# Turning the last two heads' attention probabilities by TensorE transposes instead of DMA transposes

## The chip, the cores and the metric

One core of one Trainium2 chip runs the whole program in one launch. The metric is the device time in microseconds (us) of one execution; a time is the median of several runs. A profile is one further execution, recorded by the hardware profiler; its times count from the start of its span. In the profile PE is TensorE (PEld its weight loads), DVE is VectorE, ACT is ScalarE, POOL is GpSimd and SP is SyncE, whose queue issues most DMAs.

## The reference

Two layers work on 256 tokens and 256 context tokens of width 2048, in float32. Layer 0 is a Fourier mixer, layer 1 an attention. The change lies in the attention, which for each of 64 query heads (8 per key head, head width 64) computes

```python
s = einsum('bqhgd,bkhd->bhgqk', q, k) * 64 ** -0.5
s = where(mask, s, NEG_INF)                # 256 own keys in a window, 256 context keys
p = softmax(concatenate([s, sink], -1))[..., :-1]
o = einsum('bhgqk,bkhd->bqhgd', p, v)
y = o * silu(z)
x = x + gate * (y @ w_out[1])              # then a final rmsnorm
```

The product with the values contracts over keys, while the softmax leaves a tile with queries on partitions. So each head's probabilities have to be turned before the second product. That is 512 keys by 256 queries for each head.

## The kernel before

**Precision.** A float32 product is done as three products of high and low parts (`mm3`, lines 77 to 80: lines 78, 79 and 80 of the profile). `split` (lines 64 to 66) makes the parts: ACT casts the high part (line 65), DVE or POOL subtracts for the low part (line 66). Probabilities and values are split into two float16 parts instead.

**One head.** `stage_s(i)` (from line 1141) computes the scores of head i for two blocks of 128 queries (lines 1154 and 1155), masks and reduces them on DVE (line 1156), exponentiates on ACT (line 1159), and writes for each block a float16 tile `f` of 128 queries by 1024, namely 512 high parts by ACT (line 1166) and 512 low parts by DVE (line 1167). Line 1168 then has SP issue one DMA transpose per block, which writes the turned tile `ft`. Tiles `f` have three buffers, and so do the tiles `ft`. `stage_o(i)` (from line 1171) multiplies by the values with 8 matmuls of 256 columns (lines 1176 and 1177), which need both blocks of `ft`; ACT and DVE take the result out (lines 1182 and 1183), and after every second head `emit_y` (line 1139) makes one block of y.

**The loop.** Head i's scores are issued two iterations ahead of its `stage_o`. Between them `filler()` issues units of other PE work: q and z projections (lines 1118 and 1120), and at the end the first 12 of 16 weight pieces of the output projection's first quarter (`o1_step`, from line 984; weights `wo1a`). That quarter reads y split in high and low parts by `y_split` (from line 976): blocks 0 to 15 into `ys` tiles of one pool, blocks 16 to 23 into tiles of the pool `act` with POOL subtracting, blocks 24 to 31 into `ys` tiles of the last stage's pool with DVE subtracting. After the loop come the last four weight pieces (lines 1246 to 1249), the exit of that quarter (`evac`, lines 1235 to 1244, which needs the gate row `gbc` and the residual tiles `x2`), and then the quarters with the weights `wo1b` and `wo1c`.

**What sets the order.** The kernel is written in a tile framework that places instructions by a model of its own: each engine's order is fixed when the program is built, and need not be that of the source. A tile's pool decides which buffer it gets. The pool `act` has 33 buffers of 128x512 float32, and at the end of the attention it holds y, the values, the parts of y's blocks 16 to 23, and the eight residual tiles `x2`, which POOL loads by DMA at line 1228. The rows `gbc` (line 1223) and `fg` (line 1230) are loaded by POOL's queue too. Weights arrive through three `raw` buffers of 1 MB (line 49), issued on SP's queue, the queue of the DMA transposes.

Of the kernel before, what the change touches and what calls it, by code (L numbers as in the profile page):

```python
# [12 lines left out]
F16 = mybir.dt.float16  # L13
# [4 lines left out]
P = 128  # L18
# [13 lines left out]
def tile_dit(ctx: ExitStack, tc: tile.TileContext, a: dict, out: bass.AP):  # L32
    nc = tc.nc
    V, S, PE, GP = nc.vector, nc.scalar, nc.tensor, nc.gpsimd
# [4 lines left out]
    actp = ctx.enter_context(tc.tile_pool(name="act", bufs=33))  # L39
    pp = ctx.enter_context(tc.tile_pool(name="ps", bufs=8, space=bass.MemoryType.PSUM))  # L40
    dram = ctx.enter_context(tc.tile_pool(name="dram", bufs=1, space=bass.MemoryType.DRAM))

    def psum():
        return pp.tile([P, 512], F32, tag="ps", name="ps")

    def raw(src, q=None):
        t = rawp.tile([P, D], F32, tag="raw", name="raw")
        n = src.shape[-1]
        last_dma[0] = (q or nc.sync).dma_start(t[:, :n], src).ins
        return t  # L50
# [3 lines left out]
    def act(dt=F32):  # L54
        return actp.tile([P, 512], dt, tag="act", name="act")
# [21 lines left out]
    def mm3(o, wh, wl, xh, xl, start, stop):  # L77
        PE.matmul(o, wh, xh, start=start, stop=False)  # L78
        PE.matmul(o, wh, xl, start=False, stop=False)  # L79
        return PE.matmul(o, wl, xh, start=False, stop=stop).ins  # L80
# [19 lines left out]
    ident = const.tile([P, P], F32, name="ident")  # L100
# [598 lines left out]
    with tc.tile_pool(name="yp", reuse_waits="tile", bufs=32) as ypool:  # L699
# [20 lines left out]
        with tc.tile_pool(name="zp", reuse_waits="tile", bufs=2) as zp:  # L720
# [30 lines left out]
            for b in range(4, NB):  # L751
# [3 lines left out]
                o = psum()  # L755
# [41 lines left out]
        for i in range(32):  # L797
            sw, kg = i // 16, i % 16
            if kg == 0:
                o = [psum() for _ in range(8)]  # L800
# [6 lines left out]
            if kg >= 12:  # L807
                for k in range(sw * 8 + (kg - 12) * 2, sw * 8 + (kg - 12) * 2 + 2):
                    t = act()
# [41 lines left out]
    with tc.issue_after(st_end[0]):  # L851
        o = psum()
# [34 lines left out]
    with tc.tile_pool(name="h1", reuse_waits="tile", bufs=16) as h1p:  # L887
# [4 lines left out]
        with tc.tile_pool(name="kvp", reuse_waits="tile", bufs=2) as kvp:  # L892
# [3 lines left out]
            for k in range(KT):  # L896
                hx = h1p.tile([P, 512], F32R, tag="h1", name="h1")
                hc = kvp.tile([P, 512], F32R, tag="h1c", name="h1c", bufs=16)
                t = kvp.tile([P, 512], F32, tag="ht", name="ht")
# [14 lines left out]
            o = [[psum() for _ in range(2)] for _ in range(4)]  # L914
# [13 lines left out]
            for tb in range(4):  # L928
                t, ab = act(), act(F32R)
# [3 lines left out]
                t = act()  # L933
# [18 lines left out]
            for tb in range(4):  # L952
                t = vs[tb][0]
# [10 lines left out]
        with tc.tile_pool(name="at", reuse_waits="tile", bufs=2) as at:  # L964
# [19 lines left out]
            def o1_step(k, os_, wh, wl):  # L984
                while len(yh) <= min(k + 4, NB - 1) and (len(yh) < 24 or fin):
                    y_split(len(yh))
                for tb in range(2):
                    mm3(os_[tb], yh[k][:, tb * P : (tb + 1) * P], yh[k][:, N + tb * P : N + (tb + 1) * P], wh, wl, k == 0, k == NB - 1)
            slot = [0]

            def k_turn(hp):
                o = psum()
                for tb in range(4):
                    PE.transpose(o[:, tb * P : (tb + 1) * P], kr[tb][:, hp * P : (hp + 1) * P], ident)
                t = act()
                S.copy(t, o)
                kT.append(t)
# [135 lines left out]
            def emit_y(blk):  # L1133
                if blk not in szs or (blk, 1) not in obs or blk in ydone:
                    return
                ydone.add(blk)
                if blk % 2 == 0:
                    y1.append(act())
                V.scalar_tensor_tensor(y1[blk // 2][:, (blk % 2) * N : (blk % 2 + 1) * N], obs[blk, 1], dsc[:, blk // 4 : blk // 4 + 1], szs.pop(blk), op0=ALU.mult, op1=ALU.mult)

            def stage_s(i):
                hk, blk, hh = i // 8, i // 2, i % 2
                p2, pr = (blk % 4) // 2, blk % 2
                kkh, kkl = kk[hk]
                q2 = qq[hk, p2][hh]
                pt = [at.tile([P, 512], F32, tag="p", name="p", bufs=3) for _ in range(2)]
                mx = at.tile([P, 2], F32, tag="mx", name="mx")
                sm = at.tile([P, 2], F32, tag="sm", name="sm")
                es = at.tile([P, 2], F32, tag="es", name="es")
                so = []  # L1150
                for tb in range(2):
                    o = psum()
                    st = q2[:, (pr * 2 + tb) * P : (pr * 2 + tb + 1) * P]
                    PE.matmul(o, st, kkh, start=True, stop=False)  # L1154
                    PE.matmul(o, st, kkl, start=False, stop=True)  # L1155
                    V.tensor_tensor_reduce(o, o, mask[:, tb, :], -0.125, nsink[:, i : i + 1], ALU.add, ALU.min, mx[:, tb : tb + 1])  # L1156
                    so.append(o)
                for tb in range(2):
                    S.activation(pt[tb], so[tb], AF.Exp, bias=mx[:, tb : tb + 1], scale=-1.0, accum_out=sm[:, tb : tb + 1])  # L1159
                S.activation(es, mx, AF.Exp, bias=sink[:, i : i + 1])  # L1160
                V.scalar_tensor_tensor(sm, sm, 1.0 / PS, es, op0=ALU.mult, op1=ALU.add)
                V.reciprocal(sm, sm)
                ft = at.tile([P, 8, 2, P], F16, tag="ft", name="ft", bufs=3)
                for tb in range(2):
                    f = at.tile([P, 1024], F16, tag="f", name="f", bufs=3)
                    S.activation(f[:, 0:512], pt[tb], AF.Copy, scale=sm[:, tb : tb + 1])  # L1166
                    V.scalar_tensor_tensor(f[:, 512:1024], pt[tb], sm[:, tb : tb + 1], f[:, 0:512], op0=ALU.mult, op1=ALU.subtract)  # L1167
                    nc.sync.dma_start_transpose(ft[:, :, tb, :], f)
                return ft

            def stage_o(i, ft):
                hk, blk, hh = i // 8, i // 2, i % 2
                oo = psum()
                for kb in range(4):
                    fh, fl = (ft[:, j, :, :].rearrange("p t q -> p (t q)") for j in (kb, 4 + kb))
                    PE.matmul(oo[:, 0:N], v01[kb][:, hk, :], fh, start=kb == 0, stop=False)  # L1176
                    PE.matmul(oo[:, 0:N], v01[kb][:, hk, :], fl, start=False, stop=kb == 3)  # L1177
                if hh == 0:
                    obs[blk, 0] = at.tile([P, N], F32, tag="ob", name="ob", bufs=4)
                ob = obs[blk, 0]  # L1180
                t = at.tile([64, N], F32, tag="ot", name="ot", bufs=1)
                S.copy(t, oo[64:128, 0:N])
                V.tensor_tensor(ob[hh * 64 : hh * 64 + 64, :], oo[0:64, 0:N], t, op=ALU.add)
                if hh == 1:
                    obs[blk, 1] = ob
                    emit_y(blk)
# [13 lines left out]
            def filler():  # L1200
                j = slot[0]
                slot[0] += 1
                emit_unit()
                if defer and defer[0][0] + 2 < j:
                    defer.pop(0)[1]()

            pts = {}
            for i in range(66):
                if i % 8 == 0:
                    while defer:  # L1210
                        defer.pop(0)[1]()
                if i < 64:
                    pts[i] = stage_s(i)
                filler()
                if i >= 2:
                    stage_o(i - 2, pts.pop(i - 2))
                filler()


        with tc.tile_pool(name="fin", reuse_waits="tile", bufs=1) as fp:  # L1220
# [31 lines left out]
            o = [[psum() for _ in range(2)] for _ in range(2)]  # L1252
# [12 lines left out]
            o = [psum() for _ in range(2)]  # L1265
# [34 lines left out]
            for kg in range(8):  # L1300
                t = raw(a["wo1c"][kg])
# [133 lines left out]
```

## Time and profile before

| | |
|---|---|
| median of 3 runs | 1819.78 us (1818.48 to 1819.86) |
| the profiled execution | 1817.29 us, span 1815.5 us |
| PE busy | 1768.6 us, 97% |
| DVE busy | 1412.0 us, 78% |
| ACT busy | 896.9 us, 49% |
| POOL busy | 212.4 us, 12% |
| DMA moved | 399.91 MB, mean 220 GB/s |
| attention's DMA transposes | 128, from 1167.4 to 1643.7 us, median 4.9 us from issue to landing |

A row of the timeline gives an instruction's start, how long it took, its engine, line and tiles, and in brackets how long the engine stood idle before it and what ended that. A row of the windows gives for a stretch of time the busy time of engines, the TensorE clock that was granted (PEclk, 1.00 is full) and the DMA rate. The page's slices are 45.4 us each.

### The profile page before, as it was taken

To read this page: it belongs to the slowest core of one execution; us is meant where nothing else is said; L and a number is where in the kernel's file an instruction comes from. 1 tells how busy PE (TensorE), PEld (TensorE's weight loads), DVE (VectorE), ACT (ScalarE), POOL (GpSimd) and SP (SyncE) were. 2 spreads that over 40 slices of the span, in tenths; PEclk is the share of its full clock that TensorE was granted. 3 is DMA by queue.
4 is the path that set the end of the run, shared out by engine and by line. 5 is a ranking of instruction groups with operands and counts; after the bars stand their busy time and mean duration, and the time that the engine had idled before them with its cause. 6 is when DMAs were issued, how large, how long until landed. Compare 5 with 4: busy or idle time off the path is not lost. (4 is left out here: it accounts for less than half of the span.)

```text
span 1815.5 us, 25987 instructions
## 1 busy us (share of the span) xinstructions
PE 1768.6 (97%) x9417; PEld 1480.2 (82%) x9417; DVE 1412.0 (78%) x2759; ACT 896.9 (49%) x1540; POOL 212.4 (12%) x213
## 2 busy tenths in 40 slices
PE   6999999999999999999999999999999999997998
PEld 4679999888888888888888888788878888875886
DVE  5679888786878887776875654899999999985455
ACT  5545454532222233324322534687778888874343
POOL 0001122100000000000001000402302231161001
PEclk9999999999999999999999999999999999998999
DMA  9988889665767647663567323587988888986553
GB/s 395 417 331 234 231 239 255 216 228 224 252 228 262 244 168 295 229 237 121 186 230 293 119 93 116 162 206 196 224 203 195 215 223 211 213 219 194 188 182 139
DMA packets 209472, 399.91 MB, mean 220 GB/s; under 512 B 156288, under 2 KB 156688, under 8 KB 174272
## 3 DMA queue, kind: packets, MB, share of 16 engines
q1 hardware_dynamic: 185280, 360.24, 61.7%
q0 software_dynamic: 19920, 31.06, 7.0%
q10 hardware_dynamic: 4144, 6.95, 1.1%
q8 instruction: 74, 1.21, 0.3%
q14 instruction: 54, 0.44, 0.1%
HBM read 352.06 MB, written 12.59 MB: 201 GB/s over the span
## 5 line engine op out<-in xcount | busy, mean ns | idle before, releaser
L65 ACT CAST wh<-raw 128x1024 fp32r<-128x1024 f32 x333 | 348.7, 1048 | 531.9 <-PE ps L79 431.1
L66 DVE TENSOR_TENSOR wl<-raw,wh 128x1024 fp32r<-128x1024 f32 x333 | 430.5, 1296 | 220.1 <-ACT wh L65 217.7
L79 PE MATMUL ps<-act,wh 128*128 128x512 f32 x1024 | 398.2, 389 | 0.0
L78 PE MATMUL ps<-act,wh 128*128 128x512 f32 x1024 | 393.8, 389 | 0.0
L80 PE MATMUL ps<-act,wl 128*128 128x512 f32 x1024 | 392.9, 389 | 0.0
L80 PEld LDWEIGHTS ps<-act,wl 128*128 128x128 f32 x1024 | 192.3, 188 | 39.8
L79 PEld LDWEIGHTS ps<-act,wh 128*128 128x128 f32 x1024 | 192.3, 188 | 39.8
L78 PEld LDWEIGHTS ps<-act,wh 128*128 128x128 f32 x1024 | 192.3, 188 | 39.7
L1118 PE MATMUL ps<-h,wh 128*128 128x512 f32 x512 | 185.5, 398 | 0.0
L686 DVE CUSTOM_DVE_ANT_0 raw<-raw,cb 128x512 f32<-128x512 f32 x256 | 172.4, 688 | 11.6 <-DMA raw<-in_adw 8.0
L686 DVE CUSTOM_DVE_ANT_0 junk<-raw,cb 128x512 f32<-128x512 f32 x192 | 131.8, 686 | 32.8 <-DMA raw<-in_adw 21.9
L1120 PE MATMUL ps<-h,wl 128*128 128x256 f32 x512 | 138.9, 281 | 0.0
L79 PE MATMUL ps<-wl,h 128*128 128x512 f32 x320 | 127.1, 397 | 0.4 <-DVE wl L66 0.4
L80 PE MATMUL ps<-wh,h 128*128 128x512 f32 x320 | 125.3, 395 | 0.0
L78 PE MATMUL ps<-wh,h 128*128 128x512 f32 x320 | 124.0, 402 | 0.0
L1167 DVE SCALAR_TENSOR_TENSOR f<-p,sm,f 128x512 f16<-128x512 f32 x128 | 102.9, 821 | 16.4 <-ACT f L1166 16.0
L1118 PEld LDWEIGHTS ps<-h,wh 128*128 128x128 f32 x512 | 96.6, 189 | 19.1
L1166 ACT ACTIVATE f<-p,sm 128x512 f16<-128x512 f32 x128 | 88.1, 717 | 41.5 <-DMA ft<-f 21.6
L1159 ACT ACTIVATE p<-ps,mx 128x512 f32<-128x512 f32 x128 | 87.9, 688 | 38.1 <-DVE mx L1156 31.6
L1120 PEld LDWEIGHTS ps<-h,wl 128*128 128x128 f32 x512 | 97.0, 190 | 2.8
L1156 DVE CUSTOM_DVE_ANT_0 ps<-ps,mask,nsink 128x512 f32<-128x512 f32 x128 | 93.4, 749 | 1.8 <-PE ps L1155 1.6
L1176 PE MATMUL ps<-ft,v 128*128 128x256 f16 x256 | 60.6, 277 | 19.7 <-DMA ft<-f 19.3
(334 smaller groups left out, 3394.9 us busy)
## 6 DMA issues: line engine op xcount, KB each, us to landing
raw<-in_wz SPq DMA_DIRECT2D x64, 1024.0 KB, 5.5
raw<-in_adw SPq DMA_DIRECT2D x64, 1024.0 KB, 5.2
raw<-in_awp SPq DMA_DIRECT2D x32, 1024.0 KB, 12.8
raw<-in_wo SPq DMA_DIRECT2D x32, 1024.0 KB, 6.1
raw<-in_wq SPq DMA_DIRECT2D x32, 1024.0 KB, 5.3
raw<-in_wu SPq DMA_DIRECT2D x32, 1016.0 KB, 6.2
raw<-in_wo1b SPq DMA_DIRECT2D x16, 1024.0 KB, 4.9
act<-in_xT POOLq DMA_DIRECT2D x32, 256.0 KB, 6.3
```

The costliest lines, as they stand in the source:

```text
L65: last_cast[0] = S.copy(h, src).ins
L66: last_sub[0] = eng.tensor_tensor(l, src, h.bitcast(F32), op=ALU.subtract).ins
L78: PE.matmul(o, wh, xh, start=start, stop=False)
L79: PE.matmul(o, wh, xl, start=False, stop=False)
L80: return PE.matmul(o, wl, xh, start=False, stop=stop).ins
L686: V.tensor_tensor_reduce(junk if s == 0 and i < 3 else wf, wf, cb[:, s, kq * 512 : kq * 512 + 512], 1.0, 0.0, ALU.mult, ALU.add, acc[:, i, ...
L1118: PE.matmul(o[0], wh[:, q], hx1[k], start=k == 0, stop=k == KT - 1)
L1120: PE.matmul(o[0][:, 0:N], wl[:, q], hx1[k][:, 0:N], start=False, stop=False)
L1156: V.tensor_tensor_reduce(o, o, mask[:, tb, :], -0.125, nsink[:, i : i + 1], ALU.add, ALU.min, mx[:, tb : tb + 1])
L1159: S.activation(pt[tb], so[tb], AF.Exp, bias=mx[:, tb : tb + 1], scale=-1.0, accum_out=sm[:, tb : tb + 1])
L1166: S.activation(f[:, 0:512], pt[tb], AF.Copy, scale=sm[:, tb : tb + 1])
L1167: V.scalar_tensor_tensor(f[:, 512:1024], pt[tb], sm[:, tb : tb + 1], f[:, 0:512], op0=ALU.mult, op1=ALU.subtract)
```

## The change

For heads 62 and 63 the DMA transposes are left out. Instead `stage_t`, issued two iterations after the head's scores, ahead of its `stage_o`, turns the float16 tile in pieces of 128x128 by 16 TensorE transposes, 8 for each block, into a float16 PSUM tile for each block; ACT copies the first block's to `ft`, DVE the second's. The identity for this, in float16, is copied once by ACT. The four `f` tiles of these heads and the identity are taken from the pool `act`, not from the three buffers of `f`. Heads 0 to 61 are turned as before.

```diff
             slot = [0]
+            ident16 = []
...
                 ft = at.tile([P, 8, 2, P], F16, tag="ft", name="ft", bufs=3)
+                fs = []
                 for tb in range(2):
-                    f = at.tile([P, 1024], F16, tag="f", name="f", bufs=3)
+                    if i < 62:
+                        f = at.tile([P, 1024], F16, tag="f", name="f", bufs=3)
+                    else:
+                        f = actp.tile([P, 1024], F16, tag="act", name="f")
+                        fs.append(f)
                     S.activation(f[:, 0:512], pt[tb], AF.Copy, scale=sm[:, tb : tb + 1])
                     V.scalar_tensor_tensor(f[:, 512:1024], pt[tb], sm[:, tb : tb + 1], f[:, 0:512], op0=ALU.mult, op1=ALU.subtract)
-                    nc.sync.dma_start_transpose(ft[:, :, tb, :], f)
-                return ft
+                    if i < 62:
+                        nc.sync.dma_start_transpose(ft[:, :, tb, :], f)
+                return ft, fs
+
+            def stage_t(ft, fs):
+                for tb in range(2):
+                    o = pp.tile([P, 8, P], F16, tag="ps", name="ps")
+                    for j in range(8):
+                        PE.transpose(o[:, j, :], fs[tb][:, j * P : (j + 1) * P], ident16[0])
+                    (S.copy if tb == 0 else V.tensor_copy)(ft[:, :, tb, :], o)
 
-            def stage_o(i, ft):
+            def stage_o(i, ft, fs):
...
+                if i == 62:
+                    t = actp.tile([P, 1024], F16, tag="act", name="ident16")
+                    ident16.append(t[:, 0:P])
+                    S.copy(ident16[0], ident)
                 if i < 64:
                     pts[i] = stage_s(i)
+                if i - 2 >= 62:
+                    stage_t(*pts[i - 2])
                 filler()
                 if i >= 2:
-                    stage_o(i - 2, pts.pop(i - 2))
+                    stage_o(i - 2, *pts.pop(i - 2))
```

In the built program the order of the engines changes with it, from about head 59 on. On PE, `stage_o` of head 61 stood behind 16 matmuls of the output projection that follow head 63's scores; now it follows those scores directly, and then come 12 of head 62's 16 transposes. The order from there is 10 matmuls, 4 transposes, 14 matmuls, `stage_o` of head 62, 8 transposes of head 63, 4 matmuls, the other 8, `stage_o` of head 63, and the remaining 20 matmuls on `act` tiles. On ACT the casts that split y's blocks 16 to 19 now stand behind head 62's line 1166, and those of blocks 20 to 23 behind head 63's; those of blocks 16 to 21 stood together ahead of both, and only the last two behind head 63's. On POOL the eight loads of `x2` now stand behind the splits of blocks 16 to 19 and ahead of those of blocks 20 to 23; seven of them stood behind the splits of 16 to 21. On SP the weight load that stood between the transposes of heads 62 and 63 follows the last `wo1a` load directly.

## The prediction

> **What bounds the kernel now.** I read the page first: which engine the slices fill, and who makes the chain that ended last.
>
> ```profile
> PE   6999999999999999999999999999999999997998
> PEclk9999999999999999999999999999999999998999
> ...
> PE 16%; DVE 4%; DMA 2%; ACT 1%; issue 1%; SPq 0%; POOLq 0%; DVEq 0%; POOL 0%; ACTq 0%
> ```
>
> PE is full in every slice but a few. The 37th (1634 to 1679 us), where the attention ends, shows 7 and the only dip of the clock, and DMA has a place in the chain. So the waits of this stretch come next, then PE's timeline and its windows.
>
> ```profile
> PE ps L1176 <- DMA ft<-f: 16.2, 2, 12.9
> ```
>
> ```profile
> 1629.14 0.28 PE L1176 MATMUL ps<-ft,v 128*128 128x256 f16 x1 [3.39 <-DMA ft<-f]
> ...
> 1629.92 0.27 PE L1177 MATMUL ps<-ft,v 128*128 128x256 f16 x1
> ...
> 1633.25 0.59 PE L78 MATMUL ps<-wh,act 128*128 128x512 f32 x1
> ...
> 1657.44 0.40 PE L1176 MATMUL ps<-ft,v 128*128 128x256 f16 x1 [12.86 <-DMA ft<-f]
> ...
> 1661.82 0.39 PE L78 MATMUL ps<-wh,ys 128*128 128x512 f32 x1
> ```
>
> From 1560 to 1665 us PE waited twice for transposes: 3.39 us ahead of head 60's `stage_o` and 12.86 us ahead of head 63's, the last. The first and last of head 60's eight matmuls start 0.78 us apart: 0.111 us each. At 1633.25 head 63's scores have just gone; at 1661.82 the first part of y's last blocks is used.
>
> ```profile
> 1169.45:1172.87 3.42, 1.41 (x12) 1.00 0.92 211
> 1172.87:1176.28 3.41, 3.41 (x12) 0.50 0.95 284
> 1623.43:1626.84 3.41, 2.33 (x11) 1.00 1.09 310
> 1626.84:1630.25 3.41, 1.11 (x9) 1.00 1.14 275
> 1630.25:1633.66 3.41, 3.41 (x9) 0.50 1.64 268
> 1657.44:1661.59 4.15, 4.15 (x15) 0.57 0.86 361
> 1661.59:1800.00 138.41, 138.41 (x598) 1.00 0.48 168
> ```
>
> The columns are the stretch, its length, PE's busy time, the clock, DMA. Two things follow. A stretch of 3.4 us in which PE was busy for only 1.41 or 1.11 us is followed by one at half clock, one with 2.33 us is not. Such a slow stretch costs 3.41 x 0.5 = 1.7 us of PE work; the one behind head 63 costs 4.15 x 0.43 = 1.8. So each long wait costs 1.7 us more than its length. And from 1661.59 to 1800 PE is busy without a gap, a 512-column matmul each 138.41 / 598 = 0.231 us: what is won ahead of this is won at the end, one for one.
>
> **Why the two waits exist.** SP's queue, POOL's queue, and three answers about landings: heads 59, 60 and 63, in this order.
>
> ```profile
> 1619.89 6.57 SPq L1168 DMA_TRANSPOSE ft<-f  x2
> ...
> 1627.28 5.37 SPq L1168 DMA_TRANSPOSE ft<-f  x2
> ```
>
> ```profile
> 1609.36 7.29 POOL L66 TENSOR_TENSOR act<-act 128x256 fp32r<-128x256 f32 x6
> 1616.60 3.82 POOL L1228 DMA_DIRECT2D act<-x1d  x7
> ...
> 1645.69 0.56 POOL L1223 DMA_DIRECT2D gbc<-gated  x1
> ```
>
> ```profile
> DMA to landing us min/median/max: 3.3/3.5/3.7
> ```
>
> ```profile
> DMA to landing us min/median/max: 7.0/7.6/8.3
> ```
>
> ```profile
> DMA to landing us min/median/max: 6.0/9.8/13.7
> ```
>
> Head 59's transposes have no POOL load beside them and land after 3.3 to 3.7 us. Head 60's are issued from 1619.89, when seven `x2` loads have just gone out from 1616.60, and take 7.0 to 8.3. Head 63's share the engines with the eighth `x2` load and with `gbc` and `fg`; the later takes 13.7. Where POOL's loads run beside them, transposes take two to four times as long.
>
> **The change, part by part.**
>
> *Head 63's wait goes:* 12.86 us, and the slow stretch behind it, 1.7. No cover is lost; what is late next is the copy out of PSUM, below.
>
> *Head 60's wait goes, though its DMA stays.* The five tiles taken from `act` (four `f`, one identity) push the splits of y's blocks 16 to 23 back. POOL's `x2` loads stand behind the first four splits, those behind ACT casts, and these behind head 62's line 1166, which ran 10 us after head 60's second transpose had gone out:
>
> ```profile
> 1622.14 4.32 SPq L1168 DMA_TRANSPOSE ft<-f  x1
> ```
>
> ```profile
> 1632.54 0.72 ACT L1166 ACTIVATE f<-p,sm 128x512 f16<-128x512 f32 x1 [0.93 <-ACT p L1159]
> ```
>
> Head 60's transposes then land like head 59's, by 1622.1 + 3.5 = 1625.6 at the latest, when PE reaches them (1629.14 - 3.39 = 1625.75). Gain 3.39 + 1.7 = 5.1 us. Bounds: 0, if the `x2` loads are not the cause, and 5.1. I take 5.1, the nearest row being head 59's.
>
> *Head 61's wait is new.* Its `stage_o` loses the 16 matmuls that covered it (16 x 0.231 = 3.7 us) and follows head 63's scores directly, at 1633.25 - 5.1 = 1628.15.
>
> ```profile
> 1625.12 0.75 DVE L1167 SCALAR_TENSOR_TENSOR f<-p,sm,f 128x512 f16<-128x512 f32 x1
> 1628.29 0.72 ACT L1166 ACTIVATE f<-p,sm 128x512 f16<-128x512 f32 x1 [5.19 <-DMA ft<-f]
> ```
>
> The first row is head 61's first block, done at 1625.87; the second block waited 5.19 us for the buffer of head 60's transposes, which now comes free in time. So its low parts follow at 1626.6 to 1627.5, and its transpose goes out at about 1627.7. With head 59's 3.5 us it lands at 1631.2 or so: a wait of 2.9 us with PE busy for some 1.4 of 3.4 us, hence one slow stretch, 1.7. Bounds of the wait: 1.6 (out at 1626.5, 3.3 us) and 8 (8.3 us as head 60's were). Behind the waiting matmul stand all of head 62's transposes and the projection; ACT and DVE work on.
>
> *32 transposes are added on PE.* The trace has float32 ones:
>
> ```profile
> 1552.63 0.60 PE L1037 MATMUL ps<-ident,act 128*128 128x128 f32 x4
> ```
>
> Four in 0.60 us with a tail of 0.27: (0.60 - 0.27) / 3 = 0.11 apart. Float16 has no row for this shape; head 60's matmuls, which load a float16 128x128 each too, are 0.111 apart. 32 x 0.11 = 3.5 us, all on PE's path, as PE has no gaps to put them in but those counted here. From below 0.8 of that (2.8), from above twice (7).
>
> *Copies.* Head 62's lie beside 14 matmuls (3.2 us): nothing. Head 63's `stage_o` stands directly behind its last transpose, so PE waits for DVE's copy of 128x1024 out of PSUM. No such row exists; the nearest are
>
> ```profile
> L65 ACT CAST wh<-raw 128x1024 fp32r<-128x1024 f32 x333 | 348.7, 1048 | 531.9 <-PE ps L79 431.1
> L66 DVE TENSOR_TENSOR wl<-raw,wh 128x1024 fp32r<-128x1024 f32 x333 | 430.5, 1296 | 220.1 <-ACT wh L65 217.7
> ```
>
> 1.05 to 1.3 us, and 0.2 for the transposes to end. DVE also has a line 66 and a line 1183 ahead of the copy, which may end late by as much as one of them. Bounds 1.3 to 2.6; I take 2.0.
>
> *ACT's identity copy and the moved casts* cost nothing: ACT had idle time here (5.19 us ahead of the row above at 1628.29), and the first of blocks 16 to 23 is used only behind head 62's transposes. If its split on POOL comes late, PE waits by the 0.9 us of a split or two.
>
> *Loads.* The four left-out DMAs free SP; PE meets `gbc` and the `wo1b` loads some 10 us earlier.
>
> ```profile
> gbc<-gated POOLq DMA_DIRECT2D x1, 1024.0 KB, 12.7
> fg<-in_fg POOLq DMA_DIRECT2D x1, 1024.0 KB, 16.4
> ```
>
> ```profile
> 1672.62 1.40 DVE L1239 TENSOR_TENSOR act<-ps,gbc 128x512 f32<-128x512 f32 x2
> ```
>
> `gbc` landed at 1645.69 + 12.7 = 1658.4 and would be wanted at 1672.6 - 9.6 = 1663.0: hidden with 4.6 us to spare. 1.8 MB of `x2` now come nearer to it, but the transposes that ran beside it are gone.
>
> *Sum.* Gone: 12.9 + 1.7 + 3.4 + 1.7 = 19.7 us. Added: 3.5 + 2.9 + 1.7 + 2.0 = 10.1. The difference is 9.6 us. From the profiled execution's 1817.3 us (span 1815.5 and 1.8 around it) that makes 1807.7. The median of the three runs, 1819.8, lies 2.5 above that execution; by it the forecast is **1810.2 us**.
>
> **The rivals.**
>
> *Transposes do not hold the clock up.* In the forecast they count as PE work. If not, the stretches after head 61's wait and after head 63's transposes fall under 1.4 of 3.4 us, and two more slow stretches follow: 2 x 1.7 = 3.4, so 1813.6 us. For it: head 63's 16 transposes stand directly before a wait. Against it: nothing, as this trace has no long run of transposes next to a wait. [...]
>
> *The second `wo1b` load is late.*
>
> ```profile
> 1647.33 0.53 SPq L49 DMA_DIRECT2D raw<-in_wo1b  x1
> ```
>
> ```profile
> DMA to landing us min/median/max: 15.0/15.0/15.0
> ```
>
> ```profile
> 1673.03 1.05 ACT L65 CAST wh<-raw 128x1024 fp32r<-128x1024 f32 x1 [1.76 <-PE ps L79]
> ```
>
> This load went out amid `gbc` and `fg`, took 15.0 us and was wanted only at 1673, by ACT's cast. Now it goes out when the last weight pieces are split, at about 1652, and is wanted at about 1663, 11 us later. At 15.0 us PE stops 4 us: 1814.2. Against it: later loads of this kind run alone, and `fg` should be in by then.
>
> *No change.* Head 60's wait stays (5.1) and head 61's runs to 8 us (5.1 more): 10.2 us against a gain of 9.6, so 1820.4. This is the case in which the `x2` loads have nothing to do with the landings.
>
> *Slower: the POOL loads, now together, starve `gbc`.*
>
> ```profile
> 1648.00:1652.00 4.00, 0.00 (x0) 0.00 (x0) 0.00 (x0) 0.00 (x0) 0.00 (x0) 0.50 1.47 122
> ...
> 1656.00:1660.00 4.00, 2.56 (x11) 1.93 (x12) 0.23 (x1) 0.64 (x2) 0.00 (x0) 0.50 0.93 383
> ```
>
> `x2`, `gbc`, `fg` and the first `wo1b` load are 5.2 MB, issued from about 1636. At the first row's 122 GB/s they take 43 us, and `gbc`, if it shares to the end, lands at 1679, 16 us behind its time. DVE stands at line 1239 with the weight splits queued behind it, and PE runs dry: 16 - 9.6 = 6.4 us lost, 1826. It decides from `gbc` landing 9.6 us late. Against it: the low rate belongs to the stretch in which head 63's transposes were in flight; 383 GB/s follow once they are landing, in the second row.
>
> That the change doesn't do what it says is excluded: the two heads have no DMA left.
>
> **How the numbers follow.** Forecast 0.66 (1805.5 to 1815 by the bounds of its terms), clock 0.10, late load 0.10, no change 0.07, slower 0.07. A measurement of this kernel tells 0.2%, about 3.6 us, from no change. The first three cases are faster by more: 0.86. Same 0.07, slower 0.07. The range 1805.5 to 1817 takes in the first three and leaves the last two out.
>
> **What would show it.** Line 1176 of head 63 waits about 2 us for DVE's copy, not 12.9 for a DMA; head 60's waits under 0.5 us and lands in under 5; head 61's waits about 3; POOL's loads at line 1228 start after 1630; the transposes are 0.11 us apart; one slow stretch rather than two. It is wrong if head 60 still waits, if head 61 waits for more than 5, or if PE stops between the last `act` matmul and `wo1c`.

## The result, and the profile after

The changed kernel takes **1803.43 us** (median of 4 runs, 1801.37 to 1805.47); the kernel before, run beside it, 1819.13 us (4 runs, 1814.29 to 1819.86). The ratio is 0.9919, with a 95% interval of 0.9901 to 0.9938. The profiled execution took 1801.37 us with a span of 1799.6, against 1817.29 and 1815.5 before: 15.9 us less. The forecast was 1810.2 (1805.5 to 1817), a gain of 9.6: the sign was right, the gain too small by 6, and the time lies under the range.

The page after, PE's slices, the clock, and the chain that ended last:

```profile
PE   6999999999999999999999999999999999999998
...
PEclk9999999999999999999999999999999999999999
...
PE 21%; ACT 1%; DVE 0%; DMA 0%; issue 0%; POOLq 0%; POOL 0%; DVEq 0%; ACTq 0%
```

The dip in the 37th slice is gone from PE and from the clock, and DMA has fallen from 2% to 0% of the chain. PE's waits from 1560 to 1665 us:

```profile
PE ps L1190 <- DVE ft L1183: 0.9, 1, 0.9
PE ps L1190 <- DMA ft<-f: 0.3, 1, 0.3
```

They were 16.2 us; now they are 1.2. The timeline of PE shows where (line 1190 is the first matmul of `stage_o`, line 1182 the transposes, line 1183 the copies):

```profile
1625.46 0.28 PE L1190 MATMUL ps<-ft,v 128*128 128x256 f16 x1
...
1628.93 0.27 PE L1190 MATMUL ps<-ft,v 128*128 128x256 f16 x1 [0.34 <-DMA ft<-f]
...
1629.80 0.83 PE L1182 MATMUL ps<-ident,f 128*128 128x128 f16 x12
...
1637.23 0.61 PE L1182 MATMUL ps<-ident,f 128*128 128x128 f16 x8
...
1638.66 0.62 PE L1182 MATMUL ps<-ident,f 128*128 128x128 f16 x8
...
1640.22 0.28 PE L1190 MATMUL ps<-ft,v 128*128 128x256 f16 x1 [0.94 <-DVE ft L1183]
```

Head 60 no longer waits, head 61 waits 0.34 us for its DMA, head 63 0.94 us for DVE's copy. Eight transposes take 0.61 us and twelve 0.83: 0.055 us from one to the next, where the forecast put 0.11. The landings of head 60's and head 61's DMA transposes, and of the eight `x2` loads, which now go out from 1632.7:

```profile
DMA to landing us min/median/max: 3.1/3.1/3.2
```

```profile
DMA to landing us min/median/max: 3.1/3.2/3.3
```

```profile
DMA to landing us min/median/max: 4.2/6.1/9.6
```

Head 60's had been 7.0 to 8.3. What the forecast did not have shows in the windows of 1609.40 to 1616.60 us, in which the kernel before ran six splits on POOL. First before, then after; the columns are the stretch, its length, then PE, PEld, DVE, ACT and POOL busy, each with its number of instructions, then the clock, the DMA share and GB/s:

```profile
1609.40:1616.60 7.20, 7.20 (x36) 5.82 (x33) 7.20 (x8) 4.85 (x12) 7.20 (x6) 1.00 0.78 206
```

```profile
1609.40:1616.60 7.20, 7.20 (x36) 5.91 (x34) 7.18 (x16) 5.17 (x13) 0.74 (x2) 1.00 0.90 251
```

DVE was busy throughout in both, but with POOL busy for only 0.74 us, not 7.20, it got 16 instructions done, not 8. The work from one head's line 1156 to the next head's took it 8.9 us before (1607.28 to 1616.22), and after, with one instruction more in it, 6.7 (line 1157, 1608.06 to 1614.74). Its groups in this stretch, before and (0.8 us later) after:

```profile
L66 DVE TENSOR_TENSOR wl<-raw,wh 128x1024 fp32r<-128x1024 f32 x2 | 3.4, 1758 | 0.0
L1167 DVE SCALAR_TENSOR_TENSOR f<-p,sm,f 128x512 f16<-128x512 f32 x2 | 1.9, 990 | 0.0
L1139 DVE SCALAR_TENSOR_TENSOR act<-ob,dsc,th 128x256 f32<-128x256 f32 x1 | 1.0, 964 | 0.0
...
L1161 DVE SCALAR_TENSOR_TENSOR sm<-sm,es 128x2 f32<-128x2 f32 x1 | 0.7, 687 | 0.0
L1183 DVE TENSOR_TENSOR ob<-ps,ot 64x256 f32<-64x256 f32 x1 | 0.4, 406 | 0.0
```

```profile
L66 DVE TENSOR_TENSOR wl<-raw,wh 128x1024 fp32r<-128x1024 f32 x3 | 3.6, 1219 | 0.0
L1173 DVE SCALAR_TENSOR_TENSOR f<-p,sm,f 128x512 f16<-128x512 f32 x3 | 2.2, 746 | 0.0
...
L1140 DVE SCALAR_TENSOR_TENSOR act<-ob,dsc,th 128x256 f32<-128x256 f32 x1 | 0.5, 481 | 0.0
L1197 DVE TENSOR_TENSOR ob<-ps,ot 64x256 f32<-64x256 f32 x1 | 0.4, 414 | 0.0
...
L1162 DVE SCALAR_TENSOR_TENSOR sm<-sm,es 128x2 f32<-128x2 f32 x1 | 0.2, 155 | 0.0
```

The same weight split took 1.76 us beside a busy POOL and 1.22 beside an idle one, the low parts of `f` 0.99 and 0.75, the product in `emit_y` 0.96 and 0.48, and an instruction on two columns (`sm`) 0.69 and 0.155. Each lost 0.24 to 0.54 us, the one on two columns (0.53) as much as the one on 1024 (0.54), so it looks more like a wait for each instruction than a lower rate. The sum into `ob`, which reads one operand from PSUM, took 0.41 both times. The four that were slowed have two inputs in SBUF; why a busy POOL slows them is not shown. The prediction had no term for it.

### The profile page after: what moved, and what is told of

Its sections match the earlier page's. It is cut to its first block, busy times and chain, and to the rows that moved or that the text cites. A ratio compares the mean times of both kernels' runs of the same rounds, so it can differ in the third digit from the quotient of the medians.

```text
span 1799.6 us, 26039 instructions
## 1 busy us (share of the span) xinstructions
PE 1765.1 (98%) x9449; PEld 1478.0 (82%) x9449; DVE 1411.3 (78%) x2761; ACT 898.3 (50%) x1543; POOL 213.5 (12%) x213
## 5 line engine op out<-in xcount | busy, mean ns | idle before, releaser
L79 PE MATMUL ps<-wl,ys 128*128 128x512 f32 (+1 forms) x192 | 75.2, 392 | 0.0
```

## The experiments

The theory behind them: what costs is a DMA transpose in flight beside a load; whatever separates the two wins the same time, and the 6 us that were not forecast come from DVE, freed of POOL's splits. The rival: the gain belongs to TensorE's turning and goes by the heads turned.

| run | median, us | range (runs) | ratio to before | 95% interval |
|---|---|---|---|---|
| `e1_x2_late` | 1804.09 | 1801.15 to 1806.25 (4) | 0.9919 | 0.9903 to 0.9936 |
| `e2_pe_turn_only` | 1808.63 | 1808.03 to 1809.37 (4) | 0.9945 | 0.9931 to 0.9960 |
| `e3_act_tiles_only` | 1819.08 | 1811.88 to 1833.66 (10) | 1.0009 | 0.9985 to 1.0032 |
| `e4_head63_only` | 1803.60 | 1802.82 to 1804.09 (4) | 0.9922 | 0.9906 to 0.9939 |
| `e5_twice` | 1801.71 | 1800.73 to 1807.88 (4) | 0.9905 | 0.9889 to 0.9922 |
| `e6_change_x2_late` | 1802.37 | 1800.93 to 1803.40 (5) | 0.9915 | 0.9900 to 0.9930 |
| `e7_x2_late_loads_held` | 1805.52 | 1803.77 to 1806.85 (6) | 0.9932 | 0.9917 to 0.9947 |
| `e8_pool_busy` | 1806.52 | 1804.31 to 1807.82 (6) | 0.9938 | 0.9924 to 0.9952 |
| `e9_dma_loads_sorted` | 1799.93 | 1799.61 to 1801.07 (4) | 0.9903 | 0.9885 to 0.9921 |
| `e10_change_loads_sorted` | 1801.80 | 1801.29 to 1803.61 (5) | 0.9913 | 0.9897 to 0.9929 |
| `e11_change_again` | 1803.00 | 1800.28 to 1806.16 (6) | 0.9919 | 0.9902 to 0.9935 |

The kernel before had medians of 1818.10, 1818.21 and 1817.74 us beside e1, e2, e3 and e5, beside e4 and e6 to e8, and beside e9 to e11.

### e8: POOL kept busy

The changed kernel, with POOL writing the low part of y's block 15 six times more; the values are the same.

```diff
+                if k == 15:
+                    for _ in range(6):
+                        GP.tensor_tensor(t[:, N : 2 * N], y1[k // 2][:, (k % 2) * N : (k % 2 + 1) * N], t[:, 0:N].bitcast(F32), op=ALU.subtract)
                 yh.append(t)
```

> The changed kernel with six more subtractions on POOL, the same result written again behind y's block 15 (128x256 each), where the kernel before had six splits and the changed kernel has an idle POOL; no other instruction moves. Theory (DVE runs slower beside a busy POOL, and this is why head 61's low parts came some 2 us earlier than forecast): DVE's line 66 goes back from 1.22 towards 1.76 us and line 1173 from 0.75 towards 0.99 in those 7 us, head 61's second transpose goes out 1.5 to 2.5 us later, its wait rises from 0.3 to 2 or 3 us, and a slow stretch of 3.4 us may follow: 1805 to 1808 us. Rival (POOL's work does not matter to DVE, the head start came from the shorter order on ACT alone): head 61 goes out as before, wait under 0.6, 1803.4 us as the changed kernel.

It took 1806.52 us, 3.5 above the changed kernel (1803.00 in e11). The ranges of their runs overlap (1804.31 to 1807.82 and 1800.28 to 1806.16), so the profile has to decide. DVE's groups from 1610.2 to 1617.4, then PE's waits:

```profile
L66 DVE TENSOR_TENSOR wl<-raw,wh 128x1024 fp32r<-128x1024 f32 x2 | 3.4, 1753 | 0.0
L1176 DVE SCALAR_TENSOR_TENSOR f<-p,sm,f 128x512 f16<-128x512 f32 x2 | 1.9, 988 | 0.0
```

```profile
PE ps L1193 <- DMA ft<-f: 3.0, 1, 3.0
PE ps L1193 <- DVE ft L1186: 0.9, 1, 0.9
```

and the stretch behind head 61's wait, with the clock in the last column but two:

```profile
1631.40:1634.80 3.40, 2.94 (x21) 2.44 (x21) 3.37 (x7) 2.59 (x6) 3.40 (x4) 0.50 0.74 284
1634.80:1638.20 3.40, 3.40 (x11) 2.73 (x10) 0.33 (x1) 1.88 (x4) 3.40 (x7) 0.58 0.40 100
```

DVE is back at 1.75 and 0.99 us, within 0.01 us of what it took in the kernel before. Head 61's second transpose goes out at 1628.56 instead of 1625.66, its wait is 3.0 us instead of 0.3, and the clock falls to half behind it. The forecast's wait for head 61 was 2.9. That e8 comes so close to it is in part luck: in e8 DVE starts head 61's low parts at 1626.42, 1.3 us later than in the kernel before (1625.12), from whose times the forecast was made. In e8 and in the changed kernel alike the second transpose goes out 2.14 us behind that start. By this an estimate for DVE's times of before is an issue at 1627.3, a landing 3.1 us later and, with PE there at 1628.6 as in the changed kernel, a wait of some 1.8 us. The theory holds, that a busy POOL makes DVE, and by it head 61's transpose, late; the rival is out.

### e5: each transpose twice

```diff
-                        PE.transpose(o[:, j, :], fs[tb][:, j * P : (j + 1) * P], ident16[0])
+                        for _ in range(2):
+                            PE.transpose(o[:, j, :], fs[tb][:, j * P : (j + 1) * P], ident16[0])
```

> The changed kernel with each of its 32 transposes done twice into the same place; the result is the same. It prices a transpose on PE's path. By the changed kernel's trace (12 in 0.83 us, 0.06 us each) 32 more cost 1.9 us; by the prediction's 0.11 us they cost 3.5 us; if they were hidden beside other waits, 0 to 1 us.

The 32 further transposes cost nothing that the median shows (1801.71 us); by their spacing they are worth 1.8, within the scatter. The profiled execution, at 1807.88 the longest of the four, is of use for another reason. PE's timeline, and its windows around a stretch at half clock:

```profile
1630.59 0.83 PE L1183 MATMUL ps<-ident,f 128*128 128x128 f16 x12
...
1641.46 0.28 PE L1191 MATMUL ps<-ft,v 128*128 128x256 f16 x1 [2.20 <-DVE ft L1184]
...
1642.72 3.21 PE L1183 MATMUL ps<-ident,f 128*128 128x128 f16 x32
```

```profile
1638.45:1641.88 3.43, 1.23 (x8) 0.72 (x7) 3.43 (x3) 1.04 (x2) 2.84 (x5) 1.00 0.93 311
1641.88:1645.30 3.42, 3.42 (x31) 3.15 (x30) 1.07 (x2) 1.00 (x2) 0.00 (x0) 0.51 1.03 426
1645.30:1648.70 3.40, 2.61 (x23) 2.19 (x22) 1.16 (x3) 1.05 (x3) 0.00 (x0) 0.99 1.00 424
```

A wait leaves PE busy for 1.23 of 3.43 us, and half clock follows. That half-clock stretch holds 0.84 us of `stage_o` and then nothing but transposes, and full clock comes back right after it. With only the 0.84 us counted it would have been below the 1.11 and 1.41 of the prediction's rows, which led to half clock. Nor does half clock end by itself after 3.4 us: in e7, below, a stretch at half clock with PE busy for 2.07 us is followed by another. So in this trace the float16 transposes count as PE work for the clock.

### e3: the tiles moved, the turning left to the DMA

The kernel before, with the tiles of heads 62 and 63 and one for the identity taken from `act` as in the change.

```diff
-                    f = at.tile([P, 1024], F16, tag="f", name="f", bufs=3)
+                    if i < 62:
+                        f = at.tile([P, 1024], F16, tag="f", name="f", bufs=3)
+                    else:
+                        f = actp.tile([P, 1024], F16, tag="act", name="f")
...
+                if i == 62:
+                    t = actp.tile([P, 1024], F16, tag="act", name="ident16")
+                    S.copy(t[:, 0:P], ident)
```

> The kernel before with heads 62 and 63 writing f into act tiles and with the identity's act tile, but turned by DMA as all others. Theory: the splits and the x2 loads move back as in the changed kernel, head 60 doesn't wait, head 61 waits under 1 us, and the gain of that half is 5 us or somewhat more; head 63's transposes now run beside all of POOL's loads, so its wait is 12.9 us or up to 4 more. In all 1 to 5 us below the kernel before, 1814 to 1818. Rival (the act tiles do nothing): as before, with head 60's wait.

Without the TensorE transposes the tiles from `act` gain nothing, where 1 to 5 us had been expected: 1819.08 us, and 22 us between the best and the worst of ten runs. PE's waits in the profiled execution (1833.66 us, the longest of the ten), how long head 63's two transposes took to land, and a stretch in the middle of it:

```profile
PE ps L1179 <- DMA ft<-f: 33.1, 3, 32.0
```

```profile
DMA to landing us min/median/max: 26.6/29.0/31.3
```

```profile
1643.80:1660.00 16.20, 0.00 (x0) 0.00 (x0) 0.00 (x0) 0.00 (x0) 0.00 (x0) 0.50 1.31 84
```

Head 63's transposes went out at 1634.91 and 1638.27, amid the eight `x2` loads (from 1632.2), with `gbc` and `fg` behind them. For 16 us no engine did anything, while the DMA engines showed themselves busy and moved 84 GB/s. So taking the tiles from `act` brings the `x2` loads down onto the last head, and the TensorE turning is what makes that harmless. By the medians the turning is worth some 15 us against this kernel.

### e1: only the loads moved

The kernel before, every head turned by the DMA, with the `x2` loads behind POOL's last split.

```diff
+                if k == 23:
+                    gp_sub[0] = last_sub[0]
...
-                    nc.gpsimd.dma_start(x2[tb][c], x1d[tb, :, c * 512 : (c + 1) * 512])
+                    with tc.issue_after(gp_sub[0]):
+                        nc.gpsimd.dma_start(x2[tb][c], x1d[tb, :, c * 512 : (c + 1) * 512])
```

> The kernel before with one edit: POOL issues the eight x2 loads behind the last of its splits (after about 1643 us) instead of at 1616.6. All turning stays with the DMA and the splits of blocks 16 to 21 stay early. Theory (x2 loads are what made head 60's transposes late): head 60's transposes land in under 5 us instead of 7.0 to 8.3, its wait of 3.4 us and the slow clock stretch behind it go, 5 us. Head 63's transposes then share the DMA with all eight x2 loads, so its wait stays at 12.9 us or grows by up to 4. In all 0 to 5 us below the kernel before. Rival (head 60 was late because DVE and POOL were slowed by the splits, not by DMA traffic): the landing of head 60's transposes stays at 7 to 8 us and the wait of 3.4 us is there; time as before.

This gained as much as the whole change, 1804.09 us, far more than was expected of it. PE's waits from 1632 to 1660, and the landings of head 60's transposes and of head 63's:

```profile
PE ps L1179 <- DMA ft<-f: 3.0, 2, 2.4
```

```profile
DMA to landing us min/median/max: 3.1/3.1/3.2
```

```profile
DMA to landing us min/median/max: 6.3/6.6/6.9
```

Head 60's part was foreseen. Head 63's wait fell with it, from 12.9 to 2.4 us, which I had not expected: with head 60 on time, head 63's second transpose goes out at 1638.48 instead of 1643.70, and the loads come behind it, the first `x2` at 1641.68 and `gbc` at 1646.94. Before, an `x2` load, `gbc` and `fg` went out 0.3, 2.0 and 2.5 us after it. The rival, that the gain belongs to the turning by TensorE alone, is out.

### e2: only the turning moved

TensorE turns the two heads, but `f` stays in its own three buffers and the identity lies in the spent constant `ng`, so the splits and the `x2` loads stay early.

```diff
-                    if i < 62:
-                        f = at.tile([P, 1024], F16, tag="f", name="f", bufs=3)
-                    else:
-                        f = actp.tile([P, 1024], F16, tag="act", name="f")
+                    f = at.tile([P, 1024], F16, tag="f", name="f", bufs=3)
+                    if i >= 62:
                         fs.append(f)
...
-                    t = actp.tile([P, 1024], F16, tag="act", name="ident16")
-                    ident16.append(t[:, 0:P])
+                    ident16.append(ng.rearrange("p a k s -> p (a k s)").bitcast(F16))
```

> The changed kernel with its f tiles from the three buffers of f and its float16 identity in a spent constant, so that no act tile is taken and the order of POOL's and ACT's splits and of the x2 loads is that of the kernel before. Theory: head 63's wait of 12.9 us is replaced by one of 1 to 2 us, but head 60's wait of 3.4 us and its slow clock stretch are back, so 5 to 6 us above the changed kernel, 10 to 11 below the kernel before (ratio 0.994). Rival (the whole gain is TensorE's turning): as the changed kernel, 0.992 or less, with no wait at head 60.

1808.63 us: some 10 gained, 5 less than by the whole change. The landings of head 60's transposes, and the wait that is left from them:

```profile
DMA to landing us min/median/max: 7.3/8.1/8.8
```

```profile
PE ps L1188 <- DMA ft<-f: 4.1, 1, 4.1
```

The `x2` loads meet head 60's DMA as before. So the turning alone is worth some 10 us, and with it in place the tiles from `act`, which put the loads and POOL's splits later, 5 more.

### e4: only head 63 turned by TensorE

```diff
-                    if i < 62:
+                    if i < 63:
...
-                if i == 62:
+                if i == 63:
...
-                if i - 2 >= 62:
+                if i - 2 >= 63:
```

> Only head 63 is turned by TensorE; head 62 goes back to the DMA, and the tiles taken from act are three, not five. The order follows: the casts of y's blocks 16 to 19 stand ahead of head 60's line 1172, the x2 loads behind the sixth split, which now stands behind head 63's low parts. Collision theory (a DMA transpose is late where a load of 1 MB moves beside it, and head 63's are the ones that met gbc and fg): head 60's land in under 4 us as nothing of POOL's is out by then, head 62's in 4 to 7 beside SP's own weight load with a wait of at most 1 us, head 63 waits about 1 us for DVE's copy; 1803 to 1806 us. Rival (each head's DMA transposes cost about the same, and the gain goes by heads turned): half the gain, about 1811 us.

1803.60 us: turning head 62 as well brings nothing that can be measured. Head 62's DMA transposes took 5.7 and 7.3 us and cost one wait of 2.9, longer than the 1 us that I had expected, but no stretch at half clock followed: head 62's eight matmuls behind it start 0.11 us apart, as head 61's do ahead of it.

```profile
PE ps L1190 <- DMA ft<-f: 2.9, 1, 2.9
```

### e7 and e9: the DMA's turning with the loads out of its way

In e1 the last two heads' transposes still took 6 to 7 us, although head 62's had no load of POOL's beside them and head 63's none until 3.2 us after the second had gone out. SP had issued a weight load of 1 MB ahead of each pair, ahead of head 63's by 0.70 us (1636.22 and 1636.92). e7 is e1 with those two loads held behind the transposes.

```diff
-                    raw1[0] = raw(a["wo1a"][n // 2])
+                    with tc.issue_after(turned[62]) if n == 14 else nullcontext():
+                        raw1[0] = raw(a["wo1a"][n // 2])
...
-                w = ws_split(raw(a["wo1b"][kg]))
+                with tc.issue_after(turned[63]) if kg == 0 else nullcontext():
+                    t = raw(a["wo1b"][kg])
+                w = ws_split(t)
```

> The kernel before with x2 late, all heads turned by DMA, and besides the two weight loads that SP issued right ahead of head 62's and head 63's transposes held back behind them (the last wo1a load and the first wo1b load); nothing else moves. In the run without this hold those transposes took 6.3 to 7.2 us with no load of POOL's beside them, head 63 waited 2.4 us and head 62 0.5, and 6.8 us at half clock followed. Collision theory in its wider form (any 1 MB load issued just ahead makes them late, SP's own too): they land in 3 to 4.5 us, both waits go and the slow stretch with them, 5 to 6 us gained: 1798 to 1800 us, under the changed kernel with no TensorE turning at all. Rival (transposes are slow for another reason, such as following each other closely): 6 to 7 us stay, waits as before, 1803 to 1805. Second rival (the held loads are then late for ACT's casts): transposes quick but waits at line 78 or 79 of 2 us or more.

Head 63's landings, DVE's first use of `gbc`, PE's wait behind it, and the two stretches in and after it:

```profile
DMA to landing us min/median/max: 3.1/3.2/3.2
```

```profile
1661.05 1.29 DVE L1245 TENSOR_TENSOR act<-ps,gbc 128x512 f32<-128x512 f32 x2 [6.82 <-DMA gbc<-gated]
```

```profile
PE ps L79 <- DVE wl L66: 3.6, 2, 3.3
```

```profile
1663.40:1666.80 3.40, 2.07 (x5) 1.71 (x6) 2.74 (x3) 2.85 (x6) 1.75 (x2) 0.52 0.02 7
1666.80:1670.20 3.40, 3.40 (x10) 2.66 (x9) 3.40 (x3) 1.05 (x1) 1.75 (x1) 0.50 0.48 152
```

The transposes became quick (head 63's 3.1 to 3.2 us, 6.3 to 6.9 in e1), so SP's own load had been what slowed them. But the time was 1805.52, no better than e1: now `gbc` took 13.3 us beside `x2` and the weight loads, DVE stood 6.8 us at its first use with the weight splits queued behind it, and PE ran dry for 3.3 us and then had 6.8 at half clock. This is the mechanism of the prediction's slower rival, in small.

e9 is e7, and besides leaves only the two `x2` loads that the first exit needs ahead of `gbc`, and puts the other six behind `fg`.

```diff
-                for c in range(4):
-                    nc.gpsimd.dma_start(x2[tb][c], x1d[tb, :, c * 512 : (c + 1) * 512])
+                with tc.issue_after(gp_sub[0]):
+                    nc.gpsimd.dma_start(x2[tb][0], x1d[tb, :, 0:512])
             fg = fp.tile([P, D], F32, name="fg")
-            nc.gpsimd.dma_start(fg, a["fg"].broadcast_to([P, D]))
+            fgd = nc.gpsimd.dma_start(fg, a["fg"].broadcast_to([P, D])).ins
+            for tb in range(2):
+                for c in range(1, 4):
+                    with tc.issue_after(fgd):
+                        nc.gpsimd.dma_start(x2[tb][c], x1d[tb, :, c * 512 : (c + 1) * 512])
```

> The kernel with x2 late and the two weight loads held (all turning by DMA), and besides only two of the eight x2 loads stay ahead of gbc on POOL's queue, the two that the first exit needs; the other six go behind gbc and fg. In the kernel without this the transposes took 3.1 to 3.9 us, but gbc took 13.3 us beside x2 and three weight loads, and PE stood 3.3 us at line 79 with 6.8 us at half clock behind it. Theory (what is left is only that gbc comes late for line 1260's kind, with the weight splits queued behind it on DVE): gbc lands in 5 to 9 us, by 1656, the 3.3 us and the slow stretch (3.4) go, 1798 to 1800 us, 3 to 5 under the changed kernel. Rival (the first weight loads of wo1b, 9 to 11 us in flight, are what the splits wait for): the wait stays and the time stays at 1804 to 1806.

```profile
PE ps L78 <- ACT ys L65: 0.8, 1, 0.8
PE ps L79 <- DVE wl L66: 0.6, 1, 0.6
PE ps L1181 <- DMA ft<-f: 0.3, 1, 0.3
PE ps L80 <- DVE ys L66: 0.2, 1, 0.2
```

```profile
1654.49 1.41 DVE L1248 TENSOR_TENSOR act<-ps,gbc 128x512 f32<-128x512 f32 x2
```

These are all of PE's waits from 1560 to 1720 us, and DVE no longer waits for `gbc`. It still took 11.6 us, so the expected 5 to 9 was wrong, but it went out at 1641.36, not 1647.61, and landed 8 us earlier. At 1799.93 us this kernel lies 18 us below the kernel before and, by the medians, 3 below the changed one, with no head turned by TensorE. Its four runs lie within 1.5 us, from 1799.61 to 1801.07. The changed kernel's shortest runs (1800.28 in e11) are as short, but others of its runs are longer, and the intervals of the two ratios overlap; so e9 is shown to be at least as good, and better only by the medians.

### e6, e10 and e11: the same for the changed kernel

e6 is the changed kernel with the lines of e1 added, e10 has e9's sorting besides, e11 is the changed kernel as it is.

> The changed kernel with the eight x2 loads behind POOL's last split, as in the run with the loads late and all turning by DMA. The built order of PE also moves 14 matmuls from behind head 63's product to ahead of it. Collision theory: with the two heads on TensorE no transpose meets the loads in either place, so nothing is gained by moving them; the wait for DVE's copy (0.9 us) is covered by the 14 matmuls: 1801.5 to 1803.5 us, at most 2 under the changed kernel. Rival (the two cures add up, since each alone gained 14 to 16 us): well under 1799. Second rival (x2, gbc and fg together, now later, leave gbc late for line 1260): line 1260 waits for gbc, PE stops some us, 1805 or more.

> The changed kernel with x2 behind POOL's last split, and six of the eight x2 loads behind gbc and fg. That kernel without the sorting had no wait for gbc longer than 1 us that reached PE. Theory: only noise and the waits of 0.6 to 1.1 us at head 61 and at lines 78 and 80 are left, nothing to gain: 1801.5 to 1803 us. Rival (late gbc and fg still cost some us in most executions): 1799 to 1801.

> The changed kernel once more beside these two, to compare on one chip: 1803.4 us within 1. All theories expect this.

1802.37 and 1801.80 us, against 1803.00. The two cures do not add up: once the two heads need no DMA, the loads have nothing left to disturb. The differences of 0.6 and 1.2 us are within the ranges of the runs and settle nothing.

## Why the prediction was wrong

**Right: the bound, the two waits and their cause.** The gone side, 19.7 us, came as forecast. Head 63's wait for a DMA is gone, head 60's too, its landing went from 7.0 to 8.3 us down to 3.1, and no stretch at half clock is left between 1560 and 1660 us of the profiled execution (PEclk 1.00 throughout). e1 and e2 put the cause where the prediction had it, in POOL's loads beside the transposes (head 60's landed in 3.1 to 3.2 us with the loads late, in 7.3 to 8.8 with them early); e7 adds SP's own weight loads, which the prediction did not name (head 63's landed in 3.1 to 3.2 us with them held, in 6.3 to 6.9 in e1).

**Wrong: the added side, 10.1 us forecast and 3.1 measured.** Term by term:

- **The step that failed: "Head 61's wait is new", 2.9 us and 1.7 of slow clock behind it.** It was 0.34, and no slow stretch. Head 61's second transpose was to go out at about 1627.7 and land by 1631.2; it went out at 1625.66 and landed at 1628.80, while PE came at 1628.6, near the forecast 1628.15; the lower bound of 1.6 us had taken the issue at 1626.5. I had carried DVE's times over from the trace of before and counted only the buffer that comes free earlier. The change also takes six splits off POOL in the 7 us ahead of it, and beside an idle POOL DVE got through twice as many instructions (16 against 8). It started head 61's low parts at 1623.52 (the row below), not 1625.12. These 1.6 us are most of the 2.0 by which the transpose went out early; for the rest, the forecast put its issue 2.6 us behind that start, and it was 2.1. It also landed in 3.1 us, not 3.5. e8 put the work back on POOL and got a wait of 3.0 us, with the half clock behind it and 3.5 us on the median. The slow stretch was not certain even with the wait: e4 had a wait of 2.9 us without one. This term is 4.3 of the 7 us.

```profile
1623.52 1.41 DVE L1173 SCALAR_TENSOR_TENSOR f<-p,sm,f 128x512 f16<-128x512 f32 x2
```

- **The transposes**, 3.5 us forecast, are 32 x 0.055 = 1.8. The float32 row that I took them from is twice as dear (0.11), and the lower bound of 2.8 was not low enough.
- **Head 63's copy**, 2.0 us forecast, is a wait of 0.94, under its lower bound of 1.3. DVE had a line 66 and a line 1197 ahead of it, as feared, but the copy itself is half to two thirds as long as the float32 rows that priced it (1.05 to 1.3 us):

```profile
1639.49 0.67 DVE L1183 COPY ft<-ps 128x1024 f16<-128x1024 f16 x1
```

With the measured terms the sum is 19.7 - 3.1 = 16.6 us; the spans differ by 15.9. At the same matmul near 1600 us the changed kernel stands 0.1 us behind (1601.62 against 1601.52), and at PE's last one 16.1 ahead (1790.42 against 1806.56). So 0.1 us of the missing 0.7 was lost before 1600 us and 0.2 behind PE's last matmul; 0.4 is not placed.

**The rivals.** *Transposes do not hold the clock up*: out, by e5, for these float16 transposes. *The second `wo1b` load is late*: it landed in 7.2 us, and no wait behind it shows. *No change*: out. *`gbc` starves*: it landed 7.4 us after its issue, at 1648.5, and DVE took it up at 1656.5 without a wait; e7 shows that the mechanism exists (DVE stood 6.8 us for `gbc`), and e9, in which DVE did not wait for it, that the order of POOL's loads decides it.

**What stays open:** why a DMA transpose and a load together move so little (84 GB/s in e3). The runs show that it is so, not the cause. Both profiled executions of the changed kernel (1801.37 and 1800.28 us) are among the shorter half of its ten in the result and e11; the other five took 1804.73 to 1806.16. What these wait for is not shown, and the terms above hold for the shorter ones. That POOL's work reaches head 61 by way of DVE and no other is shown in e8 only as far as DVE's durations and the time of issue moved together.

## What to carry to other kernels

When a wait for a transfer is on the path, ask first what shares its time: here moving the loads, holding two back and sorting the rest by when they are needed gave at least as much as replacing the transfer (medians 1799.9 against 1803.0 us). And when a change moves work off one engine, re-time the engines beside it in that stretch, and don't carry their durations over.

## What the runs showed of the hardware that I had not expected

- Four kinds of DVE instructions, each with two inputs in SBUF, took 0.24 to 0.54 us longer beside a busy POOL (1.76 against 1.22 us for 128x1024, 0.99 against 0.75 for 128x512, 0.96 against 0.48 for 128x256, 0.69 against 0.155 for 128x2); one with an operand in PSUM did not (0.41).
- Float16 transposes of 128x128 followed each other every 0.055 us in the changed kernel (float32 ones 0.11 in the kernel before), and DVE copied 128x1024 float16 out of PSUM in 0.67 us.
- A pair of DMA transposes landed in 3.1 to 3.2 us (head 60's in the changed kernel and in e1, head 63's in e7), in 6.3 to 6.9 when a 1 MB load had gone out on their own queue 0.70 us ahead (head 63's in e1), in 7.0 to 8.8 beside POOL's `x2` loads (head 60's in the kernel before and in e2), and in 26.6 to 31.3 amid `x2`, `gbc` and `fg` (head 63's in the longest execution of e3).
- In e5 a 3.4 us stretch at half clock that held 0.84 us of matmuls and 2.6 of transposes was followed by full clock (0.99). In e7 one in which PE was busy for only 2.07 us was followed by another at half clock (0.50); in the kernel before one at full clock with 2.33 us was followed by full clock.
